# A hybrid delta-rule and S5 decoder layer: whole tiles for the small products, and the FFN's norm factor from sums of products

## The chip, the cores and the metric

The kernel runs on one core of one Trainium2 chip. The metric is the device time of one execution, in microseconds. TensorE multiplies a 128x128 tile of weights with a stream of columns; VectorE, ScalarE and GpSimd do the rest; transfers are issued by the queues of SyncE, ScalarE and GpSimd.

## The reference

One layer on 256 prompt tokens and 64 sample tokens (8 sequences of 8), D = 2048, all in float32. The part of it that the change touches:

```python
q = l2norm(q) * (DN_HEAD_DIM ** -0.5); k = l2norm(k)             # 8 heads of 128
...
u = einsum(tinv, v * beta);  w = einsum(tinv, k * beta * exp(gcum))
v_new = u - w @ s
o = (q * exp(g)) @ s + attn @ v_new
s = s * exp(g_last) + (k * exp(g_last - g)).T @ v_new            # per sample sequence
o = rmsnorm(o, g_dn_out) * silu(z)
...
mix = concatenate([o, y5]) @ w_out
x = x + gt1 * rmsnorm(mix, g_post_mix)
h = rmsnorm(x, g_pre_ffn) * (1 + sc2) + sh2
f = (silu(h @ w_gate) * (h @ w_up)) @ w_down
x = x + gt2 * rmsnorm(f, g_post_ffn)
```

`rmsnorm` divides by the root of the mean square over the 2048 features of a token. The FFN is 5632 wide.

## The kernel before

Features lie on the partitions, tokens on the free axis: 16 tiles of 128 features by N = 320 columns (256 prompt, 64 sample). Every large product is made with three matmuls per weight tile (`mm3`): ScalarE rounds a weight tile to a high part (`whi`, L501), VectorE subtracts to get the low part (`wlo`, L502), and the activations are split in the same manner. Raw weight tiles of 128x1024 come in on SyncE's queue (`load`, L472) into 12 slots that raw, high and low parts share.

The order is written by a planner. A list `items` fixes the main sequence of weight segments: input projection, conditioning products (`ps_ax<-raw,cs`, 32-wide), GLU, output projection first over the S5 features and then, in 16 chunks of 128 outputs, over the 8 heads, then the FFN in four blocks of 11 column chunks with the down projection behind each. Between the matmuls of a segment a planner with a clock for every engine and queue (`tick`, `bg`) drops in the instructions of background generators when it reckons them ready. On an engine all instructions run in the order in which they were recorded.

The places that the change touches:
- `conv` (L1056): 16 feature chunks of q and k; each adds its sum of squares to one row of a shared bank with a matmul on `ohc`, a column of ones that is moved along 64 columns, so 32 output rows.
- `samples` and `sample(h)` (L2008): per head, transposes of k and v to 64 rows, two products with the 64x64 matrices in `LAs`, state products of `kd` (64 rows of tile `kr`) with masked values in `Z` and `sP`, and a transpose of the outputs back.
- The second half of the output projection (`second_half`, L2200): per chunk, `post_chunk` (L2302) adds the halves on VectorE, squares and sums on GpSimd (`sqt`, `sqa`), and scales by `gm` on ScalarE (prompt) and GpSimd (samples).
- `residual` (L2332): when 14 chunks are through, the sum over the partitions by a matmul on `onesc`, Ln and exp (`rs2`), then for 16 tiles `M*rs2 + xr` (`res_pair`, two tiles on VectorE, one on GpSimd), a square on ScalarE and a matmul each on `x1s`, Ln and exp (`rs3`). `modulate2` (L2367) then makes the FFN's input tile by tile.
- `ffn` (L2389): the first two column chunks of gate and up run over four feature tiles at a time (banks bA and bB), so that they can start before all 16 tiles are there; all other chunks use eight at a time.
- `add_rows` (L2507), `output` (L2514): transposes of the result by 128 columns, and the last 64 columns by a 64-row product.

While `quiet` is set in `residual`, the planner splits no weights ahead.

## Time and profile before

| | |
|---|---|
| median of 3 runs | 1849.12 us (1849.0 to 1851.51) |
| the profiled execution | 1848.28 us, span 1846.5 us |
| mean granted TensorE clock | 0.981 of full speed |
| busy: PE, DVE, ACT, POOL | 95%, 52%, 41%, 17% of the span |
| chain that ended last, by engine | PE 76%, DVE 7%, DMA 5%, POOL 4%, ACT 4% |

In the rows below PE is TensorE's matmuls, PEld its weight loads, DVE VectorE, ACT ScalarE, POOL GpSimd. A float32 matmul stands as two records, since it takes two passes. Matmuls overlap in the pipeline, so their pace is read from start to start, not from durations. In brackets at a row's end stands the idle time ahead of it and what ended it.

### The profile page before, as it was taken

Reading aid. Unit: us, or ns where it says so; the run is one execution under the profiler, and the core shown is the slowest. Engines: PE = TensorE matmul, PEld = TensorE weight load, DVE = VectorE, ACT = ScalarE, POOL = GpSimd, SP = SyncE. Lnnn points to the kernel's source line nnn. Section 1 sums busy time; section 2 is a strip of 40 time slices with the busy share of each in tenths; the row PEclk is TensorE's granted clock in tenths of the full one; section 3 lists DMA queues with packets and bytes.
Section 4 is the critical chain, followed back from the end, with each engine's and each line's share of the span. In section 5 each row is a group of like instructions: output and inputs, shape, how many; then the busy total and the mean of one; then the engine's idle time right before and its main releaser. Section 6 shows DMA issues by size and latency. Waiting matters only on the chain.

```text
span 1846.5 us, 32677 instructions
## 1 busy us (share of the span) xinstructions
PE 1756.6 (95%) x12971; PEld 1597.3 (87%) x12971; DVE 963.8 (52%) x1806; ACT 757.9 (41%) x1422; POOL 316.6 (17%) x429
## 2 busy tenths in 40 slices
PE   6899998898899899998999999999999999999998
PEld 4677996676787677896899999999999999999997
DVE  3577843878756357555744334444444434444455
ACT  3433334575744246433533334333333333333343
POOL 1000084656031221035400000000000000000043
PEclk9899999999999999998999999999999999999999
DMA  8899744676858946866665566554565545655452
GB/s 275 274 362 295 191 120 135 197 205 191 270 152 246 271 142 188 270 168 206 204 192 150 158 183 183 150 148 120 151 176 150 151 121 156 177 149 149 124 146 85
DMA packets 501263, 340.66 MB, mean 184 GB/s; under 512 B 45356, under 2 KB 452620, under 8 KB 500782
## 3 DMA queue, kind: packets, MB, share of 16 engines
q1 hardware_dynamic: 483904, 332.41, 61.1%
q10 hardware_dynamic: 16838, 5.93, 1.3%
q8 instruction: 102, 1.67, 0.4%
q14 instruction: 51, 0.41, 0.1%
q0 software_dynamic: 368, 0.24, 0.1%
HBM read 323.22 MB, written 14.54 MB: 183 GB/s over the span
## 4 chain that ended last, share of the span: by engine, by line
PE 76%; DVE 7%; DMA 5%; POOL 4%; ACT 4%; issue 2%; SPq 1%; ACTq 0%; POOLq 0%; DVEq 0%
PE ps_mm L319 37%; PE ps_bA L319 20%; PE ps_bB L319 14%; PE ps_ax L319 2%; DMA raw<-in_w_in_dram 2%; POOL bx L281 2%; DVE wlo L502 2%; POOL AB L281 1%; ACT whi L501 1%; DVE ca L306 1%; DMA hist<-in_state_conv_dram 1%; DMA ts<-ts 1%; SPq L472 1%; PE ps_bB L333 1%; DVE acc L281 1%
## 5 line engine op out<-in xcount | busy, mean ns | idle before, releaser
L502 DVE TENSOR_TENSOR wlo<-raw,whi 128x1024 fp32r<-128x1024 f32 (+2 forms) x441 | 501.3, 1140 | 568.7 <-ACT whi L501 345.8
L501 ACT ACTIVATE whi<-raw 128x1024 fp32r<-128x1024 f32 (+2 forms) x441 | 424.4, 965 | 434.4 <-DVE wlo L502 316.3
L319 PE MATMUL ps_mm<-h,whi 128*128 128x320 f32 x1344 | 296.4, 308 | 0.0
L319 PE MATMUL ps_mm<-hT,whi 128*128 128x320 f32 x1204 | 288.7, 326 | 3.9 <-ACT hT L264 1.5
L319 PEld LDWEIGHTS ps_mm<-h,whi 128*128 128x128 f32 x1344 | 224.6, 187 | 0.8 <-issue 0.8
L319 PEld LDWEIGHTS ps_mm<-hT,whi 128*128 128x128 f32 x1204 | 201.5, 193 | 25.8 <-issue 16.6
L319 PE MATMUL ps_mm<-h,wlo 128*128 128x320 f32 x672 | 206.7, 308 | 0.0
L319 PE MATMUL ps_mm<-hT,wlo 128*128 128x320 f32 x602 | 190.1, 316 | 3.1 <-DVE wlo L502 3.1
L319 PE MATMUL ps_bA<-h,whi 128*128 128x320 f32 x736 | 163.6, 309 | 1.9 <-ACT whi L501 1.9
L319 PE MATMUL ps_bB<-h,whi 128*128 128x320 f32 x736 | 162.6, 308 | 0.0
L319 PE MATMUL ps_mm<-f,whi 128*128 128x320 f32 x704 | 155.5, 308 | 0.0
L281 POOL TENSOR_TENSOR sqa<-acc 128x320 f32<-128x320 f32 x1 | 0.7, 720 | 852.0 <-DVE acc L281 852.0
L319 PEld LDWEIGHTS ps_bA<-h,whi 128*128 128x128 f32 x736 | 124.1, 189 | 2.1 <-ACT whi L501 2.1
L319 PEld LDWEIGHTS ps_mm<-h,wlo 128*128 128x128 f32 x672 | 125.9, 187 | 0.0
L319 PEld LDWEIGHTS ps_bB<-h,whi 128*128 128x128 f32 x736 | 122.9, 187 | 1.7 <-issue 1.7
L319 PEld LDWEIGHTS ps_mm<-hT,wlo 128*128 128x128 f32 x602 | 115.7, 192 | 5.5 <-DVE wlo L502 5.4
L319 PEld LDWEIGHTS ps_mm<-f,whi 128*128 128x128 f32 x704 | 117.2, 187 | 0.8 <-ACT whi L501 0.8
L319 PE MATMUL ps_bA<-h,wlo 128*128 128x320 f32 x368 | 114.0, 310 | 0.7 <-DVE wlo L502 0.7
L319 PE MATMUL ps_bB<-h,wlo 128*128 128x320 f32 x368 | 113.2, 308 | 0.0
L319 PE MATMUL ps_mm<-f,wlo 128*128 128x320 f32 x352 | 108.4, 308 | 0.4 <-DVE wlo L502 0.4
L319 PE MATMUL ps_ax<-raw,cs 128*32 128x512 f32 (+2 forms) x832 | 99.1, 587 | 7.5 <-DMA raw<-in_w_ada_dram 7.5
L319 PE MATMUL ps_mm<-hx,whi 128*128 128x320 f32 x328 | 82.6, 338 | 6.4 <-ACT whi L501 6.4
(554 smaller groups left out, 2857.2 us busy)
## 6 DMA issues: line engine op xcount, KB each, us to landing
raw<-in_w_ada_dram SPq DMA_DIRECT2D x180, 512.0 KB
raw<-in_w_gate_dram SPq DMA_DIRECT2D x88, 512.0 KB
raw<-in_w_up_dram SPq DMA_DIRECT2D x88, 512.0 KB
raw<-in_w_in_dram SPq DMA_DIRECT2D x66, 512.0 KB
raw<-in_w_down_dram SPq DMA_DIRECT2D x64, 512.0 KB
raw<-in_w_out_dram SPq DMA_DIRECT2D x32, 512.0 KB
raw<-in_w_down_dram SPq DMA_DIRECT2D x64, 192.0 KB
raw<-in_w_glu_dram SPq DMA_DIRECT2D x16, 512.0 KB
```

Of the source, the lines that this page charges most:

```text
L281: return e.tensor_tensor(out, a, b, op=op)
L306: return self.V.scalar_tensor_tensor(out, a, s, b, op0=op0, op1=op1, **kw)
L319: return self.T.matmul(out, lhsT, rhs, start=start, stop=stop)
L333: return self.T.transpose(out, in_, self.ident[b:b + p, b:b + p])
L472: return self.nc.sync.dma_start(s.raw[:, :w].rearrange("p (k c) -> p k c", c=s.ncol), src)
L501: return (self.S.activation(s.hi[:, :w], s.raw[:, :w], AF.Copy), self.V.tensor_tensor(s.lo[:, :w], s.raw[:, :w], s.hi[:, :w].bitcast(F32), ...
L502: self.V.tensor_tensor(s.lo[:, :w], s.raw[:, :w], s.hi[:, :w].bitcast(F32), op=OP.subtract))
```

## The change

1. `ohc` grows to 256 columns, and the norm products of `conv` give 128 rows.
2. `LAs` gets 128 rows, the lower 64 cleared by GpSimd; the two matrices of a head change places, and each product takes both of them as one 128x128 tile. `kr` has its columns 0 to 128 cleared in the lower 64 rows, so that the state products take 128 rows; the outputs move to columns 128 to 256 of the lower rows, and their transpose becomes a 128-row product with half an identity. The transposes of k and v take 128 columns.
3. Between the two norms: with `M` the scaled output of a chunk, `xr` the input and `rs2` the first factor, the sum of `(M*rs2 + xr)^2` is `rs2^2 * sum(M^2) + 2 * rs2 * sum(M*xr) + sum(xr^2)`. The three sums are gathered: `sum(xr^2)` once at the start (`ssx`), the others per chunk in `mix_chunk`. `residual` then needs six matmuls on `onesc` (three sums up to chunk 14, three last chunks), three on `ssx`, and a chain of five VectorE instructions on one tile (`ms`). `M*rs2 + xr` is made in `modulate2`, the add on VectorE for the first four tiles (`QUIET` is 4) and on GpSimd for the others.
4. In the FFN, column chunk 2 of gate and up comes forward, eight feature tiles at a time behind the second and the fourth group of four.
5. The transposes of the output take 128 columns (64 of them twice), and rows 64 to 128 are stored. A scratch area for transfers that GpSimd describes shrinks from 4096 to 2048.

```diff
-            yield from self.p.mm(self.ssps[:32, :N], self.ohc[:, 31 - ch:63 - ch], a[:, :N], ch == 0, ch == 15)
+            yield from self.p.mm(self.ssps[:, :N], self.ohc[:, 127 - ch:255 - ch], a[:, :N], ch == 0, ch == 15)
...
-        self.LAs = self.bp.tile([64, 8, 2, 64], F32, name="LAs", tag="s5m")
+        self.LAs = self.bp.tile([128, 8, 2, 64], F32, name="LAs", tag="s5m")
+        self.G.memset(self.LAs[64:128], 0.0)
...
+        self.G.memset(kr[64:128, 0:128], 0.0)
...
-        yield from self.p.tr(ps[:64, 256:384], x[:, 16 + h, 256:N])
-        yield from self.p.tr(ps[:64, 384:512], x[:, 8 + h, 256:N])
+        xf = x.rearrange("p c w -> p (c w)")
+        w = xf.shape[1] // 24
+        for c, o_ in ((16 + h, 256), (8 + h, 384)):
+            n = 128 if c < 23 else 64
+            yield from self.p.tr(ps[:n, o_:o_ + 128], xf[:, c * w + 256:c * w + 256 + n])
...
-        yield from self.p.mm(ps[:64, 128:256], self.LAs[:, h, 1, :], R)
+        both = self.LAs[:, h].rearrange("p k i -> p (k i)")
+        yield from self.p.mm(ps[:, 128:256], both, kr[:, 128:256])
...
-        yield from self.p.mm(ps[64:128, 128:256], self.LAs[:, h, 0, :], R)
+        yield from self.p.mm(ps[:, 128:256], both, kr[:, 128:256])
...
-                yield from self.p.mm(pu[:, j * 256:j * 256 + 256], kd, vm[j])
+                yield from self.p.mm(pu[:, j * 256:j * 256 + 256], kr[:, 0:128], va[j])
...
-        yield from self.p.tr(pz[:, 0:64], o, b=64)
+        yield from self.p.mm(pz[:, 0:64], kr[:, 128:256], self.ident[:, 64:128])
...
+    def mix_chunk(self, m, ps):
+        M = self.M[m]
+        yield from self.p.add(M, ps[:, :N], M)
...
+        t, u, w = (self.xw(n)[:, :N] for n in ("sqt", "xm", "mq"))
...
+        yield from self.p.act(t, M, AF.Square)
+        yield from self.p.act(M[:, :NP], M[:, :NP], AF.Copy, scale=gm[:, 0:1])
...
+        yield from self.p.mul(s, s, gm[:, 1:9, None].to_broadcast([128, 8, 8]), eng=self.G)
...
+        yield from self.p.mul(u, M, self.xr[m][:, :N])
+        yield from self.p.act(w, M, AF.Square)
...
+            for a, b, e in zip(self.sums, (t, u, w), (self.G, self.V, self.G)):
+                yield from self.p.add(a, a, b, eng=e)
...
-        yield from self.rs_bcast("rs2")
-        rs = self.rsr
-        self.x1ps = self.bank("bA")
-        for m in range(0, KT, 3):
-            self.res_pair(range(m, min(m + 2, KT)), rs, self.V)
-            if m + 2 < KT:
-                self.res_pair((m + 2,), rs, self.G)
-        for m in range(KT):
-            t = self.xw("x1s")
-            self.act(t[:, :N], self.M[m], AF.Square)
-            self.mm(self.x1ps[:, :N], self.onesc, t[:, :N], m == 0, m == KT - 1)
...
+        for i in range(3):
+            yield from self.p.mm(b[i][:, :N], self.onesc, self.sums[i], True, False)
...
+        for i in range(3):
+            yield from self.p.mm(b[i][:, :N], self.onesc, self.last[i], False, True)
...
+        yield from self.p.mul(v, b[2][:, :N], rs)
+        yield from self.p.stt(v, b[1][:, :N], 2.0, v, OP.mult, OP.add)
+        yield from self.p.mul(v, v, rs)
+        yield from self.p.add(v, v, px[:, :N])
+        yield from self.p.ts(v, v, 0.0, OP.max)
...
+    def modulate2(self, kt, rm, rs):
...
+        yield from self.p.mul(x, x, rm)
+        yield from self.p.add(x, x, self.xr[kt][:, :N], eng=self.V if kt < self.QUIET else self.G)
...
+            if k0 % 8:
+                segs.append(Seg(wg, k0 - 4, 8, 256, 128, lambda s: gu(s, "g", 2, ("mm",))))
+                segs.append(Seg(wu, k0 - 4, 8, 256, 128, lambda s: gu(s, "u", 2, ("mm",))))
...
-        self.mm(p2[:64, cs], x[:, NP:N], self.ident, start and m % 4 == 0, not start and m % 4 == 3)
+        self.mm(p2[:, cs], x[:, NP - 64:N], self.ident, start and m % 4 == 0, not start and m % 4 == 3)
...
-    nc = bacc.Bacc("TRN2", target_bir_lowering=False, num_devices=1, dynamic_dma_scratch_size=4096)
+    nc = bacc.Bacc("TRN2", target_bir_lowering=False, num_devices=1, dynamic_dma_scratch_size=2048)
```

On TensorE, at the passage from the output projection to the FFN, the order was as follows (`hz` is a head's output split in two, `raw,cs` the conditioning products, `adaev` their transposes, `x1s` the squares of the residual):

```order
L319 MATMUL ps_mm<-hz,wlo 128x320
L319 MATMUL ps_ax<-raw,cs 32x512 x8
L319 MATMUL ps_bA<-sqa,onesc 128x320
L319 MATMUL ps_ax<-raw,cs 32x512 x8
L319 MATMUL ps_bA<-sqt,onesc 128x320
L319 MATMUL ps_bA<-x1s,onesc 128x320 x16
L333 MATMUL ps_mm<-ident,adaev 128x128 x4
L319 MATMUL ps_ax<-raw,cs 32x512 x16
L333 MATMUL ps_mm<-ident,adaev 128x128 x4
```

and is now:

```order
L319 MATMUL ps_ax<-raw,cs 32x512 x8
L319 MATMUL ps_bB<-ident,ssx 128x128 x2
L319 MATMUL ps_bB<-ident,ssx 128x64
L319 MATMUL ps_ax<-raw,cs 32x512 x8
L319 MATMUL ps_bA<-sqt,onesc 128x320
L319 MATMUL ps_bA<-xm,onesc 128x320
L319 MATMUL ps_bA<-mq,onesc 128x320
L319 MATMUL ps_bA<-sqt,onesc 128x320
L319 MATMUL ps_bA<-xm,onesc 128x320
L319 MATMUL ps_bA<-mq,onesc 128x320
L333 MATMUL ps_mm<-ident,adaev 128x128 x4
```

The 16 matmuls on `x1s` are gone, and six on the gathered sums and three small ones on `ssx` stand where two stood.

On VectorE, the end of the projection's second half and the start of the passage were as follows (`M` and `u` are names of output tiles, `rs` with a number is the first factor):

```order
L281 TENSOR_TENSOR M<-ps_mm,M 128x320
L502 TENSOR_TENSOR wlo<-raw,whi 128x1024
L281 TENSOR_TENSOR M<-ps_mm,M 128x320 x3
L306 SCALAR_TENSOR_TENSOR amod<-mod,gv 128x144
L281 TENSOR_TENSOR M<-ps_mm,M 128x320
L281 TENSOR_TENSOR u<-u,rs_9448 128x320 x2
L281 TENSOR_TENSOR u<-u,xr 128x320 x2
L281 TENSOR_TENSOR u<-u,rs_9448 128x320 x2
L281 TENSOR_TENSOR u<-u,xr 128x320 x2
```

In the same half there stand now, behind the adds on `M`, products with the input and their sum (`xm`):

```order
L502 TENSOR_TENSOR wlo<-raw,whi 128x1024
L281 TENSOR_TENSOR M<-ps_mm,M 128x320
L281 TENSOR_TENSOR xm<-M,xr 128x320
L281 TENSOR_TENSOR M<-ps_mm,M 128x320
L281 TENSOR_TENSOR xm<-xm 128x320 x2
L281 TENSOR_TENSOR xm<-M,xr 128x320
L281 TENSOR_TENSOR M<-ps_mm,M 128x320
L281 TENSOR_TENSOR xm<-xm 128x320
L281 TENSOR_TENSOR xm<-M,xr 128x320
L281 TENSOR_TENSOR xm<-xm 128x320
```

and the passage begins:

```order
L281 TENSOR_TENSOR M<-ps_mm,M 128x320
L281 TENSOR_TENSOR xm<-M,xr 128x320
L281 TENSOR_TENSOR ms<-ps_bA,rs_9563 128x320
L306 SCALAR_TENSOR_TENSOR ms<-ps_bA,ms 128x320
L281 TENSOR_TENSOR ms<-ms,rs_9563 128x320
L281 TENSOR_TENSOR ms<-ms,ps_bB 128x320
L299 TENSOR_SCALAR ms<-ms 128x320
L281 TENSOR_TENSOR u<-u,rs_9563 128x320
L281 TENSOR_TENSOR u<-u,xr 128x320
L281 TENSOR_TENSOR u<-u,rs_9563 128x320
L306 SCALAR_TENSOR_TENSOR h2t<-u,amod,rs_9564 128x256
```

The multiply and add per tile now stand behind the chain on `ms`, in among the FFN's input (`h2t`), and the products `xm` stand ahead of it, between the weight splits.

## Rows read from the trace of the kernel before

**Rows 1.** TensorE and the others by stretch: length, busy us (instructions) of PE, PEld, DVE, ACT, POOL, clock, DMA

```profile
300.00:500.00 200.00, 175.46 (x1485) 132.55 (x1484) 149.37 (x265) 128.40 (x350) 86.34 (x112) 0.95 0.73 209
600.00:660.00 60.00, 49.28 (x847) 37.05 (x846) 24.26 (x60) 17.93 (x35) 11.82 (x20) 0.94 0.74 219
660.00:784.00 124.00, 121.63 (x900) 99.76 (x900) 74.81 (x191) 67.16 (x186) 15.53 (x28) 0.99 0.73 217
784.00:850.00 66.00, 66.00 (x452) 65.92 (x450) 31.98 (x40) 24.92 (x32) 30.77 (x44) 1.00 0.64 184
875.00:884.00 9.00, 5.67 (x42) 2.46 (x39) 8.81 (x21) 6.08 (x17) 7.34 (x20) 0.95 0.85 272
884.00:893.00 9.00, 9.00 (x57) 7.37 (x57) 7.32 (x14) 5.30 (x12) 8.22 (x16) 0.86 0.82 246
893.00:1823.00 930.00, 929.62 (x6347) 924.45 (x6346) 395.40 (x463) 334.00 (x435) 38.88 (x58) 1.00 0.54 152
```

**Rows 2.** Timeline of TensorE at the passage: start us, us, engine, line, out<-in, shapes, count

```profile
849.88 0.30 PE L319 MATMUL ps_mm<-hz,wlo 128*128 128x320 f32 x1
...
883.06 0.61 PE L319 MATMUL ps_bA<-h,wlo 128*128 128x320 f32 x1 [0.72 <-DVE wlo L502]
```

**Rows 3.** Timeline of TensorE around one product of the q and k norms

```profile
335.46 0.30 PE L319 MATMUL ps_mm<-hx,wlo 128*128 128x320 f32 x1
335.70 0.72 PE L319 MATMUL ps_bB<-ca,ohc 128*32 128x320 f32 x2
336.35 0.56 PE L319 MATMUL ps_mm<-hT,whi 128*128 128x320 f32 x2
```

**Rows 4.** 4 us of the squares between the norms: length, PE busy (instructions), PEld, ACT, clock

```profile
870.00:874.00 4.00, 4.00 (x16) 2.85 (x15) 2.29 (x6) 1.00 0.00 0
```

**Rows 5.** Groups of TensorE instructions by shape: count | busy us, mean ns | idle before

```profile
L319 PE MATMUL ps_bB<-ca,ohc 128*32 128x320 f32 x32 | 12.8, 483 | 7.1 <-POOL ca L281 7.1
L319 PE MATMUL ps_bA<-Z,kr 64*128 64x256 f32 x32 | 11.7, 445 | 0.0
```

**Rows 6.** Timeline of TensorE around the products of one sample head

```profile
737.48 0.31 PE L319 MATMUL ps_mm<-hT,wlo 128*128 128x320 f32 x1
737.72 0.43 PE L319 MATMUL ps_bA<-kr,LAs 64*64 64x128 f32 x2
738.08 0.71 PE L319 MATMUL ps_bA<-ch,xcat 128*128 128x128 f32 x4
...
741.06 0.31 PE L319 MATMUL ps_mm<-hT,wlo 128*128 128x320 f32 x1
741.30 0.70 PE L319 MATMUL ps_bA<-Z,kr 64*128 64x256 f32 x2
...
742.36 0.49 PE L319 MATMUL ps_bA<-ch,L 128*128 128x128 f32 x2
```

**Rows 7.** Timeline of ScalarE at the passage

```profile
855.40 0.53 ACT L264 ACTIVATE rs<-ps_bA,cc 128x320 f32<-128x320 f32 x1
...
875.10 0.47 ACT L264 ACTIVATE rs<-rs 128x320 f32<-128x320 f32 x1
```

**Rows 8.** Timeline of VectorE at the passage

```profile
856.53 2.24 DVE L281 TENSOR_TENSOR u<-u,rs 128x320 f32<-128x320 f32 x2 [5.82 <-ACT rs L264]
...
868.05 0.88 DVE L281 TENSOR_TENSOR M<-M,rs 128x320 f32<-128x320 f32 x2
...
881.76 1.25 DVE L502 TENSOR_TENSOR wlo<-raw,whi 128x1024 fp32r<-128x1024 f32 x1
```

**Rows 9.** Page, then groups between 784 and 850 us: VectorE and GpSimd

```profile
L502 DVE TENSOR_TENSOR wlo<-raw,whi 128x1024 fp32r<-128x1024 f32 (+2 forms) x441 | 501.3, 1140 | 568.7 <-ACT whi L501 345.8
...
L502 DVE TENSOR_TENSOR wlo<-raw,whi 128x1024 fp32r<-128x1024 f32 x18 | 24.6, 1367 | 23.0 <-ACT whi L501 19.8 <-issue 1.7 <-ACT u L264 1.5
...
L281 POOL TENSOR_TENSOR sqa<-sqa,sqt 128x320 f32<-128x320 f32 x14 | 13.2, 941 | 1.1
...
L281 POOL TENSOR_TENSOR sqt<-M 128x320 f32<-128x320 f32 x7 | 5.0, 721 | 6.4 <-DVE M L281 6.4
...
L281 POOL TENSOR_TENSOR M<-M,gm 128x64 f32<-128x64 f32 x7 | 3.0, 441 | 0.0
```

More of the change, by code (lines that the diff above doesn't have):

```diff
@@ L572, in setup @@
         self.V.memset(self.onesc, 1.0)
-        self.ohc = cp.tile([128, 64], F32, name="ohc")
+        self.ohc = cp.tile([128, 256], F32, name="ohc")
         self.V.memset(self.ohc, 0.0)
-        self.V.memset(self.ohc[:, 31:32], 1.0)
+        self.V.memset(self.ohc[:, 127:128], 1.0)
         self.cc = cp.tile([128, 8], F32, name="cc")
@@ L609, in setup @@
         self.setup_x()
+        self.ssx = cp.tile([128, 3], F32, name="ssx")
+        self.cpy(self.ssx, ss[:, 0:3])
         self.act(ss[:, 3:6], ss[:, 0:3], AF.Ln, scale=1.0 / D, bias=self.c_eps)
@@ L1719, in gram_s @@
         for k, o in ((1, Gs), (0, D)):
-            yield from self.p.mul(self.LAs[:, 4 * q:4 * q + 4, k, :], v[:, :, k], o)
+            yield from self.p.mul(self.LAs[:64, 4 * q:4 * q + 4, 1 - k, :], v[:, :, k], o)
         self.give("xw", 2)
@@ L1953, in invert_s @@
         cols = lambda o, h: slice(o * 256 + h * 64, o * 256 + h * 64 + 64)
-        U = self.LAs[:, 4 * q:4 * q + 4, 1, :]
+        U = self.LAs[:64, 4 * q:4 * q + 4, 0, :]
         yield from self.take("xw", 5)
@@ L2206, in second_half @@
             self.pend += 1
-            self.bg(self.post_chunk(m, ps, 2), front=True)
+            self.bg(self.mix_chunk(m, ps), front=True)
         self.items += [Seg(wo, 0, 8, m * 128, 128, lambda s, m=m: second_half(s, m)) for m in range(16)]
@@ L2330, in rs_bcast @@
         yield
+    def mix_chunk(self, m, ps):
+        M = self.M[m]
+        yield from self.p.add(M, ps[:, :N], M)
+        self.pend -= 1
+        yield
+        t, u, w = (self.xw(n)[:, :N] for n in ("sqt", "xm", "mq"))
+        gm = self.gm[:, m, :]
+        yield from self.p.act(t, M, AF.Square)
+        yield from self.p.act(M[:, :NP], M[:, :NP], AF.Copy, scale=gm[:, 0:1])
+        s = M[:, NP:].rearrange("p (b i) -> p b i", i=8)
+        yield from self.p.mul(s, s, gm[:, 1:9, None].to_broadcast([128, 8, 8]), eng=self.G)
+        while "xr" not in self.flags:
+            yield
+        yield
+        yield from self.p.mul(u, M, self.xr[m][:, :N])
+        yield from self.p.act(w, M, AF.Square)
+        yield
+        if m == 0:
+            self.sums = t, u, w
+            self.nsum = 1
+            return
+        while self.nsum == 0:
+            yield
+        if m == KT - 1:
+            self.last = t, u, w
+        else:
+            for a, b, e in zip(self.sums, (t, u, w), (self.G, self.V, self.G)):
+                yield from self.p.add(a, a, b, eng=e)
+        self.nsum += 1
@@ L2348, in residual @@
-        self.quiet = False
-        yield
-        self.quiet = self.QUIET > 0
-        r = self.xw("rs3")
-        yield from self.p.act(r[:, :N], self.x1ps[:, :N], AF.Ln, scale=1.0 / D, bias=self.c_eps)
-        yield from self.p.exp(r[:, :N], r[:, :N], scale=-0.5)
-        yield
+        px, b = self.bank("bB"), [self.bank("bA") for _ in range(3)]
+        for t in range(3):
+            p = 128 if t < 2 else 64
+            self.mm(px[:, t * 128:t * 128 + p], self.ssx[:p, t:t + 1].to_broadcast([p, 128]), self.ident[:p, :p])
@@ new lines, in residual @@
+        while self.nsum < KT - 1:
+            yield
+        for i in range(3):
+            yield from self.p.mm(b[i][:, :N], self.onesc, self.sums[i], True, False)
+        while self.nsum < KT:
+            yield
+        for i in range(3):
+            yield from self.p.mm(b[i][:, :N], self.onesc, self.last[i], False, True)
+        yield
+        rs, r, v = (self.xw(n)[:, :N] for n in ("rs2", "rs3", "ms"))
+        yield from self.p.act(rs, b[0][:, :N], AF.Ln, scale=1.0 / D, bias=self.c_eps)
@@ L2355, in residual @@
+        yield from self.p.exp(rs, rs, scale=-0.5)
+        yield from self.p.mul(v, b[2][:, :N], rs)
[3 more added lines that the diff above has]
+        yield from self.p.ts(v, v, 0.0, OP.max)
+        yield from self.p.act(r, v, AF.Ln, scale=1.0 / D, bias=self.c_eps)
+        yield from self.p.exp(r, r, scale=-0.5)
         self.h2 = {}
-        self.bg([self.modulate2(m, r) for m in range(KT)], k=4, front=True)
+        self.bg([self.modulate2(m, rs, r) for m in range(KT)], k=4, front=True)
@@ L2439, in ffn @@
             for f in range(f0, f1):
[L2440 removed]
+                if f < 3:
                     continue
@@ L2549, in output @@
             for t in range(3):
-                n = 128 if t < 2 else 64
+                r = slice(0, 128) if t < 2 else slice(64, 128)
                 o = self.mp.tile([128, 512], F32, name="yo", tag="h", bufs=self.hbufs)
-                (self.cpy if q == 3 and t == 1 else self.copy)(o[:n], (pt[t] if t < 2 else p2)[:n])
+                (self.cpy if q == 3 and t == 1 else self.copy)(o[r], (pt[t] if t < 2 else p2)[r])
                 dst = self.O["y_prompt"][0, t * 128:(t + 1) * 128, cols] if t < 2 else \
                     self.O["y_sample"].rearrange("b t d -> (b t) d")[:, cols]
-                self.dma(dst, o[:n])
+                self.dma(dst, o[r])
 def merge(a, b):
```

16 lines of the change are left out of this document (5 added, 11 removed).

## The prediction

> **What bounds the kernel now.** I read the span cut into stretches first, then TensorE's own timeline where the change touches it, and last the other engines around the start of the FFN. By stretch [rows 1] TensorE's idle time is very uneven: in 893 to 1823 us (the FFN) it is idle for 0.4 of 930 us, in 784 to 850 (second half of the output projection) not at all, in 660 to 784 for 2.4 of 124. Between 300 and 500, where the conv work lies, it is idle for 24.5 of 200, so another engine or a transfer ends some of the waits there. The large hole is the passage from the output projection to the FFN: the last projection matmul starts at 849.88, and the first FFN matmul on a low half (wlo) at 883.06 [rows 2], 33.2 us later. So a microsecond saved on TensorE counts nearly in full after 660, about by half around 300 to 500; and a microsecond cut from the chain through the passage counts in full until the next thing is late.
>
> The profiled execution took 1848.28 us (span 1846.5), 0.84 below the median of the runs. The sum is made against 1848.28; no more is added for the median.
>
> **Full tiles for the q and k norms.** These 16 matmuls become 128 rows by 128 columns with the same 320 columns streamed, so they take no more passes. What goes is the price of leaving and entering the full tile. Rows: the wlo matmul before starts at 335.46, the two ohc passes at 335.70, the next matmuls at 336.35 [rows 3]. On full tiles the one and the two would need 0.147 (the FFN's pitch: 930 us for 6347 records [rows 1]) and twice some 0.26 (16 passes of x1s in 4.00 us [rows 4]), together 0.67; the rows show 0.89, and the return costs about another 0.1 in the next pair, which lasts 0.56. That is 0.31 each, 5.0 us for 16 (32 records, two to a product [rows 5]). They lie in the stretch in which TensorE is 88% busy; I take half: **-2.5 us** (0 to -5).
>
> **Full tiles for the sample heads.** For each of the 8 heads: two products with LAs, two pairs of state products (Z and sP against kr), one last transpose. Around an LAs product [rows 6]: 737.48 to 738.08 is 0.60, of which 0.147 is the matmul before and two passes of 128 columns are 0.21 (0.26 times 128/320, twice), leaving 0.24. A pair of state products: 741.06 to 742.36 is 1.30, four passes of 256 columns are 0.85 and the matmul before 0.15, leaving 0.30. I call the first 0.27 and the second 0.32 with the return into the main stream. 16 of the one are 4.3, 16 of the other (32 records of Z,kr [rows 5], two to a product, and a product with Z and one with sP to a pair) 5.1, and 8 transposes at 0.15 another 1.2: 10.6 us. The widened x transposes stand beside 32-wide products that stay, so I count nothing for them. About seven tenths lie where TensorE has no other idleness (660 to 784): **-7.5 us** (+1 to -10.6; above zero because each head gets one more clear on GpSimd, and because the order moves). That move is the second price: in the order, main matmuls now stand about 190 later against the delta chain's last transposes, so the chain has 60 rather than 250 main matmuls, some 9 us (60 times 0.147) rather than 37, before the first projection matmul on a head. I count no stall for it, but keep up to 5 us in the range.
>
> The Trainium skill speaks against this edit: its page "TensorEngine Tiling (Array Packing)", section Theoretical Speedup, says that small matrices packed as several tiles of the array run at the same time. No row here shows such an overlap for the products that are widened: within a head each waits for the one before. The same page's Key Properties say that a change of tiling mode drains the engine, which is what the 0.24 to 0.31 look like. Were the first true here, the heads would give nothing, the 1840.5 of rival (b).
>
> **Passage to the FFN.** Removed: 16 pairs of multiply and add, 16 squares and 16 matmuls on them between the two norms. Before, Ln of the first factor starts at 855.40 and the second norm is ready at 875.10 + 0.47 = 875.57 [rows 7]. After: three more full matmuls (0.53 each) and three small ones stand ahead of the first Ln, so the first factor comes at about 858.3, 2 later than before (855.40 + 1.0); a chain of five VectorE instructions of about 0.45 (two of 320 in 0.88 [rows 8]) is 2.2; Ln and exp 1.0: the second norm at 861.5, **14.1 earlier**. The pair work is not gone, only moved behind the norm. Before, the first wlo split starts 6.2 after the norm (881.76 [rows 8]); now VectorE has 8 more instructions of 0.44 for the first four tiles (3.5, of which 1.0 falls into the wait for Ln), and GpSimd runs beside it (1.3): 10.0 after 861.5, first wlo matmul at 872.8 instead of 883.06, 10.3 earlier. Then TensorE wants tiles 4 to 7 after 48 matmuls and 8 small passes (8.1), at the clock of 0.86 that 884 to 893 shows [rows 1] 9.4 later, at 882.2. Their add is on GpSimd now. VectorE needs 1.8 each (6.2 over four tiles, less two small instructions that are not theirs, and 0.44), with up to 0.7 more where that add is in its way; I take 2.3, and four wlo splits of 1.25 fall between: 871.5 + 9.2 + 5 = 886. A stall of about 3.8 follows. Behind that the 14 us of early column chunk 2 (96 matmuls at 0.147) cover tiles 8 to 15. Net **-6.5 us**; the ends are -10.3 (no stall) and 0 (VectorE and GpSimd one after the other throughout). That 9 us with VectorE 98% and GpSimd 82% busy exists in 875 to 884 [rows 1] says that the small products there do run side by side, so I stay nearer the first end.
>
> **Second half of the projection.** What left the passage lands here: per chunk one product and one running sum on VectorE (0.44 each), two squares on ScalarE (0.47 each, the exponent's duration [rows 7]; 15 us more on its 25 of 66 [rows 1]) and a second running sum on GpSimd where the square was. Two instructions with both inputs in SBUF do not run side by side on VectorE and GpSimd: two took 2.24 while GpSimd ran the same, 0.88 alone [rows 8]; so a GpSimd instruction holds VectorE up for some 0.7. In 16 chunks of 24 matmuls (3.52 each at 0.147, 56 us) must then fit: 16 wlo at 1.14 (18.2), 31 new instructions of 0.44 (13.6), and on GpSimd 30 sums at 0.72 (the square's) to 0.94 and 16 scalings of 0.44 at most [rows 9]: 60 to 67 us. That is 4 to 11 too much, if nothing runs side by side. But wlo runs ahead of its use: in the order the last one stands ahead of the adds of the last four chunks, so I count two chunks (7 us) of lead; and the scalings and adds on PSUM don't all collide; wlo already goes from 1.14 to 1.37 here [rows 9] and TensorE doesn't stop. A late wlo stops TensorE; a late sum delays the norm. I take **+1.5 us** (0 to +8).
>
> **Small things.** The last product sum waits behind the wide transposes of the residual: -0.7 (0 to -2). Extra clears, the ssx copy, one wait more on the transfer of x (now needed at the first chunk): +0.5 (0 to +2). The smaller scratch for transfers is far from the path: nothing, at worst 1.
>
> Sum: 1848.3 - 2.5 - 7.5 - 6.5 + 1.5 - 0.7 + 0.5 = **1833.1**, rounded to 1833.
>
> **Rivals.** (a) Everything is gained: norms -5, heads -10.6, FFN start -10.3, the end -1, chunks 0: 1848.3 - 26.9 + 0.5 = 1822. For it: TensorE's solid rows. Against: the stall at tiles 4 to 7. (b) The heads' gain turns into a wait: the samples are a chain of short products and mask and copy steps, so TensorE merely waits longer for DMA, ScalarE or the delta chain; 600 to 660 with 10.7 us idle [rows 1] speaks for it. Without -7.5: 1840.5. (c) The FFN doesn't start sooner in effect, since tiles 4 to 7 bind: without -6.5: 1839.5. (d) Slower: VectorE and GpSimd lock each other in the 16 projection chunks. If each pays the durations that stand under contention (wlo 1.37, the two sums on GpSimd 0.94 each and the scaling 0.44 [rows 9], and the new product and sum at 0.9 each, twice 0.44), a chunk takes 1.37 + 1.8 + 2.3 = 5.5 against TensorE's 3.52: 2 us in each, 32 in all, less the 7 of the lead, 25; and the total is 1833 - 1.5 + 25 = 1856.5. It decides from about 5.3 a chunk, where it has eaten the other gains and 0.2% more. Against it: half of these durations are waiting already, and the same wait isn't paid by both.
>
> On (d) the Trainium skill, page "SBUF — State Buffer", section Who interferes with whom, has a rule: a VectorE instruction with two SBUF inputs and a GpSimd instruction that reads SBUF exclude each other for the whole instruction. The trace agrees in the pairs at 2.24. By the rule the whole excess of 4 to 11 us would be paid, less the lead: 0 to 4 us on the time, which is not (d) but lies inside the range.
>
> **How the numbers follow.** Chances: the sum (own range 1827 to 1839) 0.42; (a) 0.15; (b) 0.18; (c) 0.13; (d) 0.12. The range 1819 to 1848 leaves out some 0.05 of the tail of (a) and most of (d). 0.2% is 3.7 us, about what a measurement of this kernel can tell from no change. Faster by more: the sum, (a), and eight tenths of (b) and (c): 0.82. Within 0.2%: the rest of these and a quarter of (d), 0.09. Slower: 0.09.
>
> **What would show it.** Right: no shorter-than-128 tiles among kr, LAs and ohc rows and gaps of 0.15 around them; second norm near 861 counted from a projection end at 850 (shifted by the gains before); first FFN wlo matmul some 23 after the last projection matmul; TensorE solid in the projection's second half. Wrong: idle TensorE before wlo in that half, a wait of over 5 us at tiles 4 to 7, a new wait before the first projection matmul on a head, or an earlier end of the heads' work with the idle time moved in front of the projection.

## The result, and the profile after

The changed kernel takes 1821.7 us (median of 4 runs, 1819.69 to 1829.38) against 1849.23; the ratio is 0.9869, 95% interval 0.9848 to 0.989, so 20 to 28 us less (the two medians alone give 0.9851). The forecast was 1833, with a range of 1819 to 1848. The profiled execution has a span of 1821.4 us, 25.1 less than before.

The page of the kernel after, busy times of the engines and the granted clock of TensorE in 40 slices:

```profile
PE 1731.8 (95%) x12961; PEld 1600.4 (88%) x12961; DVE 987.7 (54%) x1840; ACT 768.9 (42%) x1439; POOL 335.0 (18%) x439
...
PEclk8999998999999989998999999999999999999998
```

TensorE is busy 24.8 us less and idle as long as before (90 us each). In sum the gain is thus TensorE time, not a closed gap. Where it lies is read from four stretches that end at the same work in both kernels: from the first product of the q and k norms to the first product of a sample head, from there to the first projection matmul on a head, the projection's second half, and from its end to the second output chunk of the FFN's down projection (its first matmul on `ps_mm`; below simply "the down projection"). Columns: stretch, its length, busy us (instructions) of PE, PEld, DVE, ACT, POOL, the granted clock, DMA share, GB/s. Before:

```profile
329.40:570.60 241.20, 223.82 (x1866) 175.69 (x1865) 177.70 (x356) 146.85 (x411) 101.72 (x133) 0.97 0.69 199
570.60:793.70 223.10, 209.08 (x2009) 167.14 (x2009) 125.57 (x312) 101.93 (x243) 34.97 (x61) 0.98 0.77 227
793.70:850.00 56.30, 56.30 (x386) 56.22 (x384) 26.76 (x32) 20.67 (x28) 30.77 (x44) 1.00 0.57 170
850.00:1050.70 200.70, 191.59 (x1251) 173.76 (x1250) 102.49 (x147) 79.34 (x128) 33.31 (x59) 0.97 0.61 180
```

After:

```profile
327.10:555.90 228.80, 215.61 (x1870) 175.58 (x1872) 179.24 (x354) 150.06 (x412) 104.91 (x136) 0.99 0.68 210
555.90:769.20 213.30, 198.10 (x2017) 169.57 (x2018) 126.40 (x314) 102.95 (x244) 38.21 (x68) 0.98 0.74 229
769.20:826.80 57.60, 56.98 (x385) 56.16 (x383) 45.39 (x61) 32.56 (x58) 36.84 (x41) 1.00 0.65 199
826.80:1025.50 198.70, 185.44 (x1233) 172.65 (x1233) 105.23 (x153) 74.05 (x113) 37.20 (x64) 0.95 0.59 182
```

The first stretch is 12.4 us shorter, the second 9.8, the third 1.3 longer, the fourth 2.0 shorter. That is 22.9; another 4.2 lie ahead of the first matmul on `hx` (219 us, after 214.5), where no product is changed yet, 2.0 are lost between there and the first stretch, and the rest up to the end is the same within 0.3. The equal idle time is a sum, too: in the first stretch it falls by 4.2 (17.4 to 13.2), in the fourth it grows by 4.2 (9.1 to 13.3). So the two stretches with the small products hold nearly everything, and the passage to the FFN, for which most of the change's code was written, holds two.

**Small products.** TensorE's timeline around a product of the norms, after:

```profile
355.00 0.31 PE L319 MATMUL ps_mm<-hT,wlo 128*128 128x320 f32 x1
355.14 0.70 PE L319 MATMUL ps_bB<-ca,ohc 128*128 128x320 f32 x2
```

The two passes on `ohc` start 0.14 after the matmul before them, where they started 0.24 after it [rows 3], and the main stream goes on between them. Around an LAs product and a pair of state products of a head, after:

```profile
722.29 0.31 PE L319 MATMUL ps_mm<-hT,wlo 128*128 128x320 f32 x1
722.44 0.38 PE L319 MATMUL ps_bA<-kr,LAs 128*128 128x128 f32 x2
722.66 0.38 PE L333 MATMUL ps_bB<-ident,ch 128*128 128x128 f32 x2
```

```profile
726.46 0.31 PE L319 MATMUL ps_mm<-hT,wlo 128*128 128x320 f32 x1
726.61 0.59 PE L319 MATMUL ps_bA<-Z,kr 128*128 128x256 f32 x2
727.04 0.59 PE L319 MATMUL ps_bA<-sP,kr 128*128 128x256 f32 x2
727.47 0.38 PE L319 MATMUL ps_bB<-ch,L 128*128 128x128 f32 x2
```

From the main matmul to the one behind the LAs product 0.37 us pass, before 0.60 [rows 6]; across the state products 1.01, before 1.30. The saving is 0.23 and 0.29 for each, against 0.24 and 0.30 that the prediction read from the rows of before.

**The passage.** TensorE, then ScalarE (the exponents of the two norm factors), then VectorE, after:

```profile
826.64 0.30 PE L319 MATMUL ps_mm<-hz,wlo 128*128 128x320 f32 x1
...
847.58 1.11 PE L333 MATMUL ps_mm<-ident,adaev 128*128 128x128 f32 x4 [8.37 <-ACT adaev L264]
848.34 0.88 PE L319 MATMUL ps_bA<-h,whi 128*128 128x320 f32 x2
850.93 0.63 PE L319 MATMUL ps_bA<-h,wlo 128*128 128x320 f32 x1 [1.71 <-DVE wlo L502]
851.36 0.73 PE L319 MATMUL ps_bA<-h,whi 128*128 128x320 f32 x2
851.89 0.47 PE L319 MATMUL ps_bA<-h,wlo 128*128 128x320 f32 x1
...
867.03 0.63 PE L319 MATMUL ps_bA<-h,whi 128*128 128x320 f32 x1 [3.03 <-DVE h L281]
```

```profile
834.60 0.47 ACT L264 ACTIVATE rs<-rs 128x320 f32<-128x320 f32 x1
...
838.24 0.47 ACT L264 ACTIVATE rs<-rs 128x320 f32<-128x320 f32 x1
```

```profile
847.30 1.08 DVE L306 SCALAR_TENSOR_TENSOR h<-h2t,mod,h 128x256 fp32r<-128x256 f32 x1
...
849.65 1.23 DVE L502 TENSOR_TENSOR wlo<-raw,whi 128x1024 fp32r<-128x1024 f32 x1
...
856.49 1.23 DVE L502 TENSOR_TENSOR wlo<-raw,whi 128x1024 fp32r<-128x1024 f32 x1 [1.55 <-issue]
858.66 1.33 DVE L502 TENSOR_TENSOR wlo<-raw,whi 128x1024 fp32r<-128x1024 f32 x1 [0.94 <-ACT whi L501]
...
866.10 0.87 DVE L281 TENSOR_TENSOR h<-h2t,h 128x64 fp32r<-128x64 f32 x1
```

Counted from the start of the last projection matmul (826.64; before 849.88 [rows 2]): the first factor is there after 8.4 us (834.60 + 0.47; before 6.5), the second after 12.1 (838.24 + 0.47; before 25.7), the first FFN matmul on a low half after 24.3 (before 33.2). Up to that matmul 8.9 us are gained. Then most of them go again. The FFN's matmuls stand 0.267 apart (851.36 to 851.89 for two), the lower of TensorE's two clock levels (1.2 GHz), behind 8.4 us without a matmul and another 1.7. The second group of four feature tiles (tiles 4 to 7, counted from 0) starts at 861.95, and at its last one, tile 7, TensorE waits another 3.03 (867.03) for the low half, which VectorE finishes at 866.97 (866.10 + 0.87); behind that TensorE is at the lower level again. The first 22 us from the first matmul on a low half, before and after:

```profile
883.00:905.00 22.00, 21.94 (x141) 20.32 (x142) 20.28 (x43) 13.02 (x28) 16.45 (x32) 0.92 0.73 217
```

```profile
850.90:872.90 22.00, 18.79 (x94) 16.67 (x95) 17.96 (x33) 9.95 (x20) 14.57 (x27) 0.74 0.39 126
```

94 matmuls instead of 141: 47 at 0.147 are 6.9 us. Of these 3.2 are the waits at tile 7 (0.15 for its high half, 3.03 for the low one). The clock accounts for most of the rest: after, 16 matmuls at the lower level take 4.4 us (850.93 to 855.36) and behind the wait 20 take 5.5 (867.03 to 872.53), 2.1 and 2.6 more than at 0.147; before, 12 take 3.3 (883.06 to 886.39), 1.6 more.

**The projection's second half.** Groups of VectorE and GpSimd in it, after:

```profile
L502 DVE TENSOR_TENSOR wlo<-raw,whi 128x1024 fp32r<-128x1024 f32 x14 | 18.4, 1311 | 11.4 <-ACT whi L501 10.6 <-ACT sqt L264 0.7
L281 POOL TENSOR_TENSOR mq<-mq 128x320 f32<-128x320 f32 x13 | 15.8, 1218 | 7.1 <-ACT mq L264 7.0
L281 POOL TENSOR_TENSOR sqt<-sqt 128x320 f32<-128x320 f32 x13 | 15.8, 1217 | 0.0
...
L281 DVE TENSOR_TENSOR xm<-xm 128x320 f32<-128x320 f32 x14 | 11.3, 805 | 0.2
```

The sums on GpSimd take 1.22 instead of 0.94 [rows 9], sums and products on VectorE 0.8 where 0.44 is their time alone, wlo 1.31. TensorE waits 0.6 us in all, 0.5 of it for VectorE's `M` and none for `wlo`.

### The profile page after: what moved, and what is told of

The parts are those of the page before. It is cut to its first block, busy times and chain, and to the rows that moved or that the text cites. A ratio compares the mean times of both kernels' runs of the same rounds, so it can differ in the third digit from the quotient of the medians.

```text
span 1821.4 us, 32727 instructions
## 1 busy us (share of the span) xinstructions
PE 1731.8 (95%) x12961; PEld 1600.4 (88%) x12961; DVE 987.7 (54%) x1840; ACT 768.9 (42%) x1439; POOL 335.0 (18%) x439
## 4 chain that ended last, share of the span: by engine, by line
PE 67%; DVE 3%; ACT 1%; issue 1%; DMA 1%; ACTq 0%; SPq 0%; DVEq 0%
PE ps_mm L319 34%; PE ps_bA L319 17%; PE ps_bB L319 14%; PE ps_ax L319 2%; DVE acc L281 1%; DVE wlo L502 1%; PE ps_bA L333 1%; ACT hT L264 0%; DVE u L281 0%; PE ps_mm L333 0%; DVE P L281 0%; DMA inv<-Y 0%; DMA raw<-in_w_ada_dram 0%; ACT whi L501 0%; DMA S<-in_state_delta_dram 0%
## 5 line engine op out<-in xcount | busy, mean ns | idle before, releaser
L319 PE MATMUL ps_mm<-h,whi 128*128 128x320 f32 x1376 | 303.4, 308 | 0.0
L319 PEld LDWEIGHTS ps_mm<-h,whi 128*128 128x128 f32 x1376 | 229.9, 187 | 0.8 <-issue 0.8
L319 PE MATMUL ps_mm<-h,wlo 128*128 128x320 f32 x688 | 211.6, 307 | 0.0
L319 PE MATMUL ps_bB<-h,whi 128*128 128x320 f32 x704 | 156.0, 309 | 0.0
L319 PEld LDWEIGHTS ps_bB<-h,whi 128*128 128x128 f32 x704 | 118.4, 189 | 0.8 <-issue 0.8
L319 PE MATMUL ps_bB<-h,wlo 128*128 128x320 f32 x352 | 108.6, 308 | 0.0
```

Source lines behind the costliest of these rows:

```text
L319: return self.T.matmul(out, lhsT, rhs, start=start, stop=stop)
```

## Experiments

Each row is against the kernel before on the same chip.

| run | ratio, 95% interval | us of some 1846 |
|---|---|---|
| whole change (the result above) | 0.9869 (0.9848 to 0.989) | -24.2 |
| norms' tiles alone | 0.9948 (0.992 to 0.9976) | -9.6 |
| heads' tiles alone | 0.9998 (0.9982 to 1.0014) | -0.4 |
| FFN norm and chunk 2 alone | 0.998 (0.9966 to 0.9993) | -3.7 |
| scratch area alone | 0.9987 (0.997 to 1.0004) | -2.4 |
| norms' and heads' tiles | 0.9905 (0.9883 to 0.9926) | -17.5 |
| whole change without heads' tiles | 0.9956 (0.9939 to 0.9973) | -8.1 |
| whole change without norms' tiles | 0.9978 (0.9962 to 0.9994) | -4.1 |
| whole change without chunk 2 | 0.9915 (0.9894 to 0.9936) | -15.7 |
| heads' tiles, inversion held back | 0.993 (0.9916 to 0.9945) | -12.9 |
| planner's cost of a tile change at 0.05 | 0.9974 (0.9961 to 0.9987) | -4.8 |
| whole change, with a fill | 0.986 (0.9834 to 0.9886) | -25.9 |
| the same, four adds on VectorE | 0.9855 (0.9835 to 0.9875) | -26.8 |

### The parts one at a time

**Norms' tiles alone** (with `ohc` at 256 columns).

```diff
-            yield from self.p.mm(self.ssps[:32, :N], self.ohc[:, 31 - ch:63 - ch], a[:, :N], ch == 0, ch == 15)
+            yield from self.p.mm(self.ssps[:, :N], self.ohc[:, 127 - ch:255 - ch], a[:, :N], ch == 0, ch == 15)
```

> The kernel before, with the 16 products of the q and k norms alone on full tiles (one column of ones moved along 256 columns, 128 output rows). Theory A, what the change saves in the first half of the span is TensorE's time for leaving and entering the full tile: 16 times 0.31 = 5.0 us, all gained, 1844. Rival B, as in the prediction, other waits take back half of it: 1846.7. Rival C, the planner lays the work of this stretch out anew and that, not the tiles, is what moves the time: more than 8 us gained, or none.

From the first norm product to the first sample head, and from there to the projection on heads:

```profile
327.70:561.00 233.30, 218.32 (x1870) 178.00 (x1872) 180.32 (x355) 149.90 (x412) 104.27 (x136) 0.98 0.70 206
561.00:787.70 226.70, 212.87 (x2009) 170.09 (x2009) 125.57 (x313) 102.34 (x244) 33.49 (x57) 0.95 0.76 224
```

In the first of the two TensorE is busy 5.5 us less than before (218.3 against 223.8): the 5.0 of the tiles, though at a clock of 0.98 instead of 0.97 a part of it can be the clock. Idle time goes from 17.4 to 15.0 as well. In the second it is 3.6 longer at a clock of 0.95. The times say 9.6 (4.4 to 14.8 by the interval), the profiled execution 6.6. Theory A fits the tiles; by the number it is theory C (more than 8), which the interval doesn't settle. All the traces together say more: in the seven kernels with these tiles the first stretch takes 228.8 to 233.3 us, in the six with the small ones (the run on the order alone left aside) 238.5 to 241.3. That is 8.7 less on average, 3.7 more than the 5.0; that this rest comes from how the planner lays out the stretch is likely, but no run separates it.

**Heads' tiles alone** (the hunks on `LAs`, `kr` and the transposes in `sample`).

> The kernel before, with the products of the sample heads alone on full tiles (LAs, kr, the last transposes). Theory A: 10.6 us of TensorE's time, all gained, 1838.6. Rival B, seven tenths gained: 1841.7. Rival C, the heads are a chain that waits for something else: 1847 to 1850.

```profile
328.20:566.70 238.50, 221.67 (x1870) 174.57 (x1873) 178.99 (x356) 147.04 (x411) 103.11 (x136) 0.98 0.70 202
566.70:792.50 225.80, 207.34 (x2018) 177.34 (x2018) 122.80 (x311) 100.83 (x242) 36.89 (x68) 0.93 0.76 223
656.00:674.00 18.00, 16.67 (x122) 14.88 (x122) 5.40 (x18) 6.38 (x15) 3.79 (x9) 0.62 0.55 172
```

No gain: rival C by the time. Where it went is in these rows. In the heads' stretch (566.7 to 792.5) TensorE is idle for 18.5 us instead of 14.0, and the clock over the stretch is 0.93 instead of 0.98; between 656 and 674 it works without much of a break at 0.62, behind the holes of the prompt chunks' inversion (`Wc`, `X`, `Y`, `T`). The scratch run below, whose program is the one of before in this stretch, has 0.96 there, so part of the clock differs from one execution to the next; the time of many executions, which shows no gain either, doesn't hang on that.

**FFN norm and chunk 2 alone** (`mix_chunk`, `residual`, `modulate2`, the early chunk).

> The kernel before, with the FFN norm factor from gathered sums and the early column chunk 2 alone; small products as before. Prediction: -6.5 at the FFN's start and +1.5 in the projection's second half, 1844. Theory A, from the trace after: the first FFN matmul on wlo comes 9 us sooner after the last projection matmul, but 7 of it go again in a stall of 3 us at the fifth feature tile and at TensorE's half clock behind both holes: net -2 and +1.3 in the projection, 1848.5.

1843.64 against 1846.78. By its trace, stretches as in the section above: the projection's second half 3.5 us longer (59.7), 24.5 us from its end to the FFN's first matmul on a low half, 8.7 less than before, and from its end 199.2 to the down projection, 1.7 less. The two stretches that this part changes are thus 1.8 us longer together, and the execution is ahead only by what lies in front of them (7.4 by 211 us, see the next run). The time lies between the two expectations; the trace sides with theory A, and that this part gains anything by itself is not shown.

**Scratch area alone** (`dynamic_dma_scratch_size=2048`).

> The kernel before, with the scratch area for transfers at 2048 instead of 4096, nothing else. The trace after is 4.2 us ahead by 213 us, before any of the changed products. Theory A: that is the spread of the weight transfers from one execution to the next, and this kernel takes the time of before (1849, within 2 us). Rival B: the smaller area makes the setup shorter, 1845.

2.4 us less, with an interval that holds no change. Its trace is 4.6 ahead by 214 us, that of the FFN norm alone, which doesn't have the smaller scratch, 7.4 ahead, those of the norms' and heads' tiles 0.2 to 0.5 behind; over all fourteen traces this point lies between 211.3 and 220.1. So the 4.2 of the changed kernel in this stretch are within what executions differ by; a small effect of the scratch isn't excluded.

### The parts together

> The kernel before with the full tiles of both the norms and the sample heads, nothing else. Alone, the norms gave some 9.5 us and the heads nothing: in that trace TensorE's saved time went into longer holes in the inversion of the prompt chunks and a granted clock of 0.93 between 567 and 792 us instead of 0.98. Theory A, the parts add: 1846.8 - 9.6 - 0.4, about 1837. Theory B, in the whole change the heads' 10.6 us come out (its trace has 198 us of TensorE in that stretch against 209 before at the same clock), so together they give more than apart: about 1828.

> The changed kernel with the sample heads as before; all else changed. If the heads give nothing (theory A): as the changed kernel, about 1822. If they give their 10.6 us in company of the other parts (theory B): about 1832.

> The changed kernel with the q and k norms' products as before; all else changed. Additive (theory A): 1822 + 9.6, about 1831. If the norms' stretch gives only the 5.0 us of its tiles and the rest belongs to how the later work is laid out: 1827.

Both kinds of tiles together, the same two stretches:

```profile
329.40:559.60 230.20, 216.74 (x1878) 176.26 (x1880) 179.10 (x355) 149.83 (x412) 104.02 (x136) 0.99 0.71 209
559.60:774.00 214.40, 199.02 (x2018) 170.19 (x2007) 125.75 (x312) 102.74 (x244) 37.94 (x67) 0.97 0.77 228
```

Theory A (the parts add) falls: apart they give 10.0, together 17.5. The intervals alone would leave little of that excess of 7.5; the traces carry it. The heads' stretch takes 214.4 us here, with TensorE busy for 199.0, as in the whole change, against 226.7 and 225.8 with either part alone. Taking the heads' tiles out of the whole change costs 16 us, taking the norms' tiles out costs 20, each far more than that part gives alone. Without the heads' tiles the heads' stretch is 223.2 again (223.1 before). The changed kernel without norms' tiles has in the heads' stretch:

```profile
566.80:785.80 219.00, 201.95 (x2018) 172.37 (x2018) 123.25 (x311) 100.56 (x242) 36.98 (x68) 0.96 0.75 232
```

219.0 us; the tiles' time is gone from "busy" at a clock of 0.96 (202.0), but 17.1 are idle.

What the pairs share is the order. Counted in main matmuls ahead of the first projection matmul on a head, the inversion of the prompt chunks (`Wc,L`) stands 480 ahead in the kernel before and with the norms' tiles alone, 477 with the heads' tiles alone, and 360 with both and in the whole change. The heads' stretch follows that: small tiles and 480, 220.6 to 226.7 us in five traces; full tiles and 477, 219.0 and 225.8 in two, so that how much this order loses isn't settled; full tiles and 360, 213.3 to 214.6 in six. The planner lays out the background work by its own clocks, among them 0.095 us for each change of tile (`retile`); fewer changes let it place things elsewhere.

### Is it the order or the tiles?

**Heads' tiles with the inversion held back.**

```diff
+        while self.cur < 211:
+            yield
         yield from self.invert()
```

> The kernel before with the sample heads' full tiles alone, and the inversion of the prompt chunks held back until segment 211 of the main sequence, which puts its products 360 main matmuls ahead of the first projection matmul on a head, as in the changed kernel (477 without the hold). Theory B, the tiles save TensorE some 10 us and the place of the inversion decides whether that comes out or is lost in holes and at the half clock: 8 to 10 us gained, about 0.995. Theory A, the heads' tiles give nothing by themselves: within 0.2% of before.

Its order has the inversion and the heads where the changed kernel has them. The heads' stretch:

```profile
564.80:778.80 214.00, 197.85 (x2017) 169.19 (x2018) 125.76 (x313) 102.70 (x244) 38.19 (x68) 0.98 0.77 228
```

214.0 us and 197.9 busy, 11.2 less than before at the same clock. Theory B: the 10.6 of the prediction's rows are there, and two lines that move the inversion turn no gain into 12.9 us.

**The order alone.**

```diff
-        t = 0.0 if k == self.tiling else 0.095
+        t = 0.0 if k == self.tiling else 0.05
```

> The kernel before with all its small tiles, but the planner's own cost of a change of tile set from 0.095 to 0.05 us, so that it lays the background work out anew: the inversion then stands 366 main matmuls ahead of the projection on heads, its last products 90 ahead, much as in the changed kernel. If the order alone is what gains in 560 to 790 us: 6 to 10 us less than before (0.995 to 0.997). If the tiles are, and the order only lets them: within 0.2% of before, or slower by a few us since more changes of tile are taken.

```profile
338.20:574.70 236.50, 226.02 (x1912) 178.03 (x1916) 177.09 (x353) 148.81 (x411) 99.14 (x135) 0.99 0.73 215
574.70:785.00 210.30, 195.93 (x1893) 154.52 (x1893) 116.00 (x301) 95.03 (x235) 33.82 (x57) 0.96 0.72 207
```

4.8 us less with all the small tiles kept (2.4 to 7.2 by the interval): between the two expectations, and the interval reaches into both. The trace of the one execution shows more: from the first matmul on `hx` (near 219) to the projection on heads 8.7 us less than before, where the run with the heads' tiles and the inversion held back shows 12.5 less. The order isn't quite that of the changed kernel (the sample heads also start later, so the two stretches cut the work a little differently). As far as that goes both count: an order of that kind is worth 5 us by itself by the times and 9 by the trace, and the heads' tiles in it 8 more (12.9 less 4.8) or 4, while in the order in which the planner puts them alone they give nothing. The split between the two stays open. Why that one order loses them is shown only as far as the rows go: more idle time around the inversion and a lower clock behind it. A kernel with exactly the changed order and small tiles wasn't run.

### The passage

**Without chunk 2.**

```diff
-            if k0 % 8:
-                segs.append(Seg(wg, k0 - 4, 8, 256, 128, lambda s: gu(s, "g", 2, ("mm",))))
-                segs.append(Seg(wu, k0 - 4, 8, 256, 128, lambda s: gu(s, "u", 2, ("mm",))))
```

> The changed kernel without the early column chunk 2 of the FFN. Prediction: that chunk (14 us of TensorE) covers feature tiles 8 to 15, of which VectorE and GpSimd make one in some 2.3 us or more; without it TensorE waits at the third and fourth group of four tiles, 5 to 8 us more. Rival: the two chunks of four tiles, 7 us of TensorE for each four, are cover enough, and nothing changes.

```profile
881.75 0.63 PE L319 MATMUL ps_bA<-h,whi 128*128 128x320 f32 x1 [2.76 <-DVE h L281]
```

The ratio is 0.0046 above the changed kernel's, 8.5 us with wide intervals; the stretch from the FFN's first matmul on a low half to the down projection is 4.7 longer (179.2 against 174.5). The wait at tile 7 is the same 3.03, and another of 2.76 stands at tile 11, the last of the third group of four, again for VectorE's `h`. The cover is needed, as the prediction had it.

**A fill, and four adds moved.**

```diff
+        for _ in range(15):
+            self.mm(b[0][:, :N], self.onesc, self.last[0], True, True)
...
-        yield from self.p.add(x, x, self.xr[kt][:, :N], eng=self.V if kt < self.QUIET else self.G)
+        yield from self.p.add(x, x, self.xr[kt][:, :N], eng=self.V if kt < 8 else self.G)
```

> The changed kernel with 15 matmuls of no use (a sum once more, into a bank that is no longer read) on TensorE behind the six sums, where it idles for 8.4 us before the FFN. Theory: that idleness drops the granted clock (0.73 between 835 and 850 us), and the FFN's first 7 us then run at half clock, so 3 to 4 us are lost; with the fill the first 24 FFN matmuls stand 0.147 apart instead of 0.267, and the time is 3 us below the changed kernel (0.985 against before). If the stall at the fifth feature tile only grows by as much as is saved, since VectorE and GpSimd set when tiles 4 to 7 are there: no change (0.987).

> As the run with the fill, and the add of feature tiles 4 to 7 on VectorE instead of GpSimd. Theory: VectorE is held up by these four GpSimd adds (it takes 1.08 for what takes 0.52 elsewhere) for 0.5 to 0.7 each, while the add costs it 0.44: the fifth tile comes about 1 us sooner and the stall of 3 us shrinks by that; 4 us below the changed kernel in all (0.9845). Rival: VectorE's list only grows, tiles 4 to 7 come later and the time is that of the fill or 1 to 2 us more.

The first 22 us of the FFN with the fill, and with the fill and the adds:

```profile
859.40:881.40 22.00, 22.00 (x136) 20.23 (x136) 19.89 (x33) 10.19 (x18) 15.80 (x25) 0.87 0.79 240
```

```profile
859.20:881.20 22.00, 21.95 (x134) 20.32 (x135) 19.15 (x35) 8.66 (x16) 14.32 (x20) 0.87 0.77 239
```

136 and 134 matmuls instead of 94, at a clock of 0.87 instead of 0.74. But it isn't the first matmuls that run faster. With the fill 1.0 and 3.1 us without one remain right ahead of the first matmul on a low half, which comes 1.3 later, and from there 22 matmuls stand 0.267 apart (6.0 us; 16 in the changed kernel). What is gone is the wait at tile 7 and the lower level behind it. With the fill, TensorE, then VectorE's low half of tile 7:

```profile
858.97 0.64 PE L319 MATMUL ps_bA<-h,wlo 128*128 128x320 f32 x1 [3.13 <-DVE wlo L502]
...
893.26 0.42 PE L319 MATMUL ps_bA<-h,whi 128*128 128x320 f32 x1 [0.34 <-DVE h L281]
...
894.34 0.41 PE L319 MATMUL ps_bA<-h,whi 128*128 128x320 f32 x1 [0.52 <-ACT h L264]
895.47 0.41 PE L319 MATMUL ps_bA<-h,whi 128*128 128x320 f32 x1 [0.71 <-DVE h L281]
```

```profile
870.17 0.22 DVE L281 TENSOR_TENSOR h<-h2t,h 128x64 fp32r<-128x64 f32 x1
```

The planner has another order for VectorE here: the low halves of tiles 5 and 6 stand ahead of three weight splits, in the changed kernel behind them, and tile 7 is complete 37.1 us after the last projection matmul (870.39 less 833.34), in the changed kernel 40.3. So the run changes two things, and it doesn't show that the hole of 8.4 us was what took the clock down. At the early column chunk 2 TensorE is 4.3 us ahead of the changed kernel, counted from the last projection matmul. Then it waits for tiles 14 and 15 (893.26 to 895.47), runs at the lower level once more, and 0.4 are left: from the end of the projection to the down projection it is 198.8 us in the changed kernel, 198.4 with the fill. With the adds on VectorE as well these waits are gone, too (tile 15 is complete 60.1 us after the last projection matmul instead of 62.1), and it is 194.8. What sets the passage's length is thus when VectorE and GpSimd have the feature tiles ready; the rival in the expectation of the fill said that, though of tiles 4 to 7.

By the times the two are 1.7 and 2.6 better than the changed kernel, inside the intervals: not shown to be faster. The fill on its own misses its expectation (3 us) by the trace; the pair meets it by the trace (4.0), by tiles 14 and 15 and not by the tile for which it was expected, and leaves it open by the times.

## Why the prediction was right, and where not

The time lies in the range, 11 below the forecast and outside the 1827 to 1839 that the prediction gave its own sum; it is the time of rival (a), 1822, but not by the way that (a) took. That the range held it is in part luck: the order, counted as nothing, gave 5 to 9 us, and the passage fell 4.5 short.

- **Price of a tile change: right.** 0.31, 0.24 and 0.30 were read; 0.23 and 0.29 came off, and TensorE's busy time fell by 5.5 (norms alone) and 11.2 (heads with the inversion held back) for 5.0 and 10.6.
- **Share of it on the path: wrong for the norms, right by luck for the heads.** The norms were taken at half because TensorE is idle for 12% there. They came out whole and more (-9.6 alone; 8.7 in the traces). Idle time of an engine next to its busy time is not time that swallows what is saved; only a wait that starts no sooner does. For the heads -7.5 was forecast; alone they gave nothing, which is rival (b); with the order changed as well, 8 (17.5 less 9.6) to 16.
- **The order: a term with the wrong sign.** The prediction saw that the chain of the prompt chunks moves behind some 190 main matmuls, counted it as nothing and kept 5 us of loss for it. It was a gain of 5 to 9 (the run on the order alone) and the condition for what the heads' tiles gave.
- **Passage, first half: right.** Second factor 13.6 sooner (14.1 forecast), first matmul on a low half 8.9 sooner (10.3); the 10.0 us of VectorE work behind the factor were 10.9.
- **Passage, second half: mis-sized.** -6.5 was forecast, -2.0 came. The wait at tiles 4 to 7 is 3.03 (3.8 forecast), but two things around it are off. Tile 7 was to be complete at 886, 36.1 us after the last projection matmul; it took 40.3. Of these 4.2 us 1.4 were lost ahead of the first low half. For the rest, the sum had the four weight splits and 2.3 a tile, but not that VectorE idles 2.7 us ahead of three of these splits (1.55, 0.94 and 0.17, the last two for ScalarE's `whi`). And it put the clock behind the wait at nothing: 20 matmuls at the lower level, 2.6 us. At tile 7's low half the changed kernel is 4.7 us ahead of the kernel before (40.4 against 45.1 after the last projection matmul), behind these 20 matmuls 2.0. The clock of 0.86 that the prediction used for the first 48 matmuls was too high as well: it has 9.4 us from the first low half to tile 4, and the kernel before itself takes 10.4 (883.06 to 893.50), the changed one 11.0. That the longer hole without the squares lowered the clock is shown for little: 16 matmuls at the lower level instead of 12, 0.5 us.
- **Second half of the projection: right in this order** (+1.5 forecast, +1.3). In the three kernels that have the same code here but not both kinds of full tiles (the FFN norm alone, the whole change without the heads' tiles, and without the norms') it is +3.5: TensorE waits 2.8 us for VectorE's adds (`M`, `u`) instead of 0.6. So the size is partly luck; and the late `wlo` that the prediction feared stopped TensorE in none of them. Rival (d) had its point of decision at 5.3 us of VectorE and GpSimd time for a chunk. The durations after add up to 5.8 or so (1.31, twice 0.8, twice 1.22, and 0.45 for the scaling), and TensorE still waits 0.6 in all. That fits the argument against (d), that the same wait stands in both engines' durations. The rule on shared ports that the Trainium skill gives ("SBUF — State Buffer", section Who interferes with whom) stood for 0 to 4 us in the prediction, and the traces agree with it in size (1.3 and 3.5).
- **End: too much.** -0.7 forecast; from the last down-projection matmul to the end it is 23.4 us, before 23.2. **Setup:** 4.2 us of the profiled gain lie there and belong to the execution as far as the runs show.
- The speedup of packed tiles that the Trainium skill gives ("TensorEngine Tiling (Array Packing)", section Theoretical Speedup; that the tiles run in parallel stands under Key Properties) would, by the prediction, have given the heads nothing. The rows after show the widened products with the same passes in less time, so no overlap was lost.

## What to carry to other kernels

A change of tile shape in the middle of a stream is paid on the matmul engine itself, a quarter to a third of a microsecond per excursion, and can be read beforehand from start-to-start gaps. Where a planner writes the order, a part tested alone says little about the part in company: look at where the long background chains land, and try the order by itself. A hole on TensorE can cost more than its length, since the work behind it runs slower: the wait of 3.03 us cost another 2.6. And when a run fills a hole, see what else its order changed: here the wait went elsewhere, because other engines made the tiles too late.

## What the runs showed of the hardware

That TensorE kept to the lower level after a hole was known from the rows of before; not expected was where it fell again. Behind 3.03 us without a matmul 20 stood 0.267 apart; behind 8.4 and 1.7 us it was 16, behind 1.0 and 3.1 it was 22, and behind three waits of 0.3 to 0.7 us (893.26 to 895.47, with the fill) another 12. And a VectorE instruction with two inputs in SBUF is stretched by a GpSimd instruction more the longer that one is: in the passage after, `h<-h2t,mod,h` takes 0.47 to 0.48 us alone, 0.47 to 0.54 beside GpSimd instructions of 64 columns (nine of them) and 1.08 to 1.11 beside those of 320 (four, one at 847.30).
